# Output-projection weights in chunk order: fewer loads, an earlier first half, turned rows in other PSUM banks, and a reworked end

## Chip, core and metric

The kernel runs on one core of a Trainium2 chip. The metric is device time in microseconds (us) of one execution; lower is better. A core has five engines with an instruction queue each: TensorE (PE, matrix products), VectorE (DVE), ScalarE (ACT), GpSimd (POOL) and SyncE (SP, which here only issues DMAs). Each engine works through its queue in order, and waits on semaphores for what the other engines or DMAs must have done.

## What is computed

The reference runs one transformer-like layer over two batches, a prompt of 512 tokens and a sample of 1024 tokens, with shared weights. Cut to what matters:

```python
h = rmsnorm(x, norm_attn_g)
z = h @ w_in                              # 1024 -> q, k, v, conv a, conv b
a_out = window_attn(q, k, v, bias, sink)  # 8 heads of 64, 2 key heads, |q-k| <= 128
c = ca * sigmoid(cb); c = dwconv31(c); c = silu(layernorm(c))
x = x + concat(a_out, c) @ w_out          # 1024 x 1024
h = rmsnorm(x, norm_ffn_g)
u = dwconv3(h @ w_up)                     # 1024 -> 2 x 2816
x = x + (silu(u[:, :2816]) * u[:, 2816:]) @ w_down
y = rmsnorm(x, norm_final_g)
```

All data is 32-bit. Every product is made from three matmuls: each operand is split into a rounded part `hi` and a rest `lo`, and hi·hi, hi·lo and lo·hi are added in PSUM. A split is one ScalarE copy (`hi`) and one subtraction on VectorE or GpSimd (`lo`).

## The kernel before

**The stages, in order of time.** First comes the input projection (its last matmul ends near 282 us), in chunks of 128 output columns; `order` lists the chunks, those from index `npr` on only for the sample (`nt` 1 and 2). Beside it, a generator `prompt_attention` (L792) runs the prompt's attention in 8 units of one block and one key head, and after it the depthwise convolution's norm. Then `prompt_out` (L798) does the prompt's output projection with `w_out` and turns the normed rows of the prompt (`make_h2`, L773; `transposed`, L236), with the first units of the sample's attention advanced between its steps. The prompt's feed-forward part follows (its last matmul at 785 us), with the sample's attention beside it, then the sample's output projection, and from about 874 us the sample's feed-forward part, written as products of 2 x 2 blocks with seven products instead of eight: up-projection in `NJ` = 22 steps (loop at L1584), down-projection in groups of 11 steps (`down_step`, L1556), and at last the final norm (`finish`, L1525).

**What sets the order.** On most stretches a planner orders each engine's queue: it simulates the instructions with a cost model and takes what is ready, by the order of the program. In the sample's feed-forward part the order of TensorE (from L1601 on also of SyncE) is that of the program (`manual_schedule`), two such blocks meeting at L1602.

**Memory.** SBUF tiles come from `Slots` (L64): named slots of fixed size, 15 of 4 KB (`q`), 4 of 4.25 KB (`c`), 61 of 2 KB (`h`), 2 of 2.25 KB (`d`). A tile gets the first free slot of the smallest size that fits, and a slot goes to the end of the list when its tile is dropped in the program. A new tile's first write waits until the last reader of the slot's earlier tile is done. PSUM is handed out the same way from 8 banks: `a0` to `a2`, `u0`, `u1`, `b0`, `b1`, `c0`; `use` says which job may take which letters. Before `prompt_out` it is set as at L830:

```python
    use.update(attn="a", norm="b", turn="ab")
```

so that turned rows (`turn`) share the `a` banks with the attention, while `out_half` takes `u` banks, and the units before it took `a` or `u`.

**Loads of `w_out`.** `load_wo(kc, n)` (L747) loads 128 rows by 512 columns of chunk `kc`, half `n`, into a 2-KB slot. For `kc` < 4 the rows of the two key heads lie apart, so there are two DMAs of 64 rows (L753); for the others one (L755). `split_wo` (L757) splits a chunk by L153 (ScalarE) and L154. `prompt_out` loads the eight chunks of a half, splits them, and runs `out_half` (L717) for each of the four blocks: per chunk three matmuls, L727 to L729, then the addition of the residual (L732) and, after half 1, the sum of squares (L739) and the scale (L137, L138). `make_h2` scales the rows (L778); `transposed` makes four transposes per 128 columns (L240) into one bank, which ScalarE (L242) and VectorE (L243) read out.

**An attention unit** (`values`, L613): `turn` transposes probabilities (L625) into a bank, ScalarE and VectorE split them from there (L627, L628); the products are L639 and L640; the result is read out by L647, L648 (ScalarE) and L649 (VectorE), and GpSimd adds the two halves (L651).

**The last up-projection step** (`j` = 21) runs seven products of 12 matmuls each (`prod`, L1156): `second`, `sixth` (its result is copied out at L1243), `seventh` (it adds to the bank that L1243 reads), the first down step's 12 matmuls, `fourth` (into a bank that ScalarE has filled with `seventh`'s result, L1252), `third`.

**The end.** For the last two row blocks (`tt` 2 and 3) of the sample, `left_first` squares the left half in advance. After the last matmul, VectorE adds the product to the rest (L1641 by way of `add`, L1036), ScalarE sums the squares (L1530), GpSimd finishes the sum (L1532) and takes the power -1/2 (L1533), VectorE and ScalarE scale the halves (L1542, L1540), and SyncE issues both stores, one after the other (L1543).

Of the kernel before, what the change touches and what calls it, by code (L numbers as in the profile page):

```python
# [99 lines left out]
def tile_hybrid_encoder(ctx: ExitStack, tc: tile.TileContext, xs, rel_bias, norm_attn_g, w_in,  # L100
# [70 lines left out]
    def want_w(i):  # L171
        if i < nch and i not in ws:
            want_raw(i)
            ws[i] = split(raws.pop(i))

# [332 lines left out]
    def load_bias(n):  # L508
        b0 = bbd[:]
        for h in range(0, NH, n):  # L510
            bt = sb.tile([n, 3 * P])
            for e in range(n):
                nc.sync.dma_start(bt[:, e, :], bass.AP(b0.tensor, b0.offset + (h + e) * NT + P - 1, [[NH * NT - 1, P], [1, 3 * P]]))
                bias.append((bt, e))
# [232 lines left out]
    def load_wo(kc, n):  # L747
        raw = wor[kc, n] = sb.tile([NT])
        s = slice(n * NT, (n + 1) * NT)
        if kc < 4:  # L750
            for kv in range(NKV):
                r0 = (kv * GRP + kc) * HD
                nc.sync.dma_start(raw[kv * HD:(kv + 1) * HD, :], w_out[0, r0:r0 + HD, s])  # L753
        else:
            nc.sync.dma_start(raw[:], w_out[0, kc * P:(kc + 1) * P, s])  # L755

    def split_wo(kc, n, dve=False):  # L757
        wo[kc, n] = split(wor.pop((kc, n)), dve)
# [63 lines left out]
    for i in range(npr, nch):  # L822
        want_raw(i + 2)
        want_w(i + 1)
        for nt in range(1, 3):
# [4 lines left out]
    use.update(attn="a", norm="b", turn="ab")  # L830
# [286 lines left out]
    class Part:  # L1117
        def __init__(self, held, n):
            self.held, self.n = held, n

        def __getitem__(self, i):
            return self.held[:, self.n, :][i]

# [100 lines left out]
    def armed(out):  # L1224

        hi, lo = A[1, 0]
# [241 lines left out]
    def mm_down(out, i, p, tt):  # L1468
        (sh, sl), (th, tl) = hl[i, p]
        c = slice(tt * P, (tt + 1) * P)  # L1470
        nc.tensor.matmul(out, sh[:, c], th[:], start=(p == 0), stop=False)  # L1471
        nc.tensor.matmul(out, sh[:, c], tl[:], start=False, stop=False)  # L1472
        nc.tensor.matmul(out, sl[:, c], th[:], start=False, stop=(p == NPAIR - 1))  # L1473
# [44 lines left out]
    def left_first(tt):  # L1518

        ss, o = early[tt] = sm(2), sb.tile([D])  # L1520
        part = cut(o11, tt)
        nc.scalar.activation(o[:, L], part, AF.Square, accum_out=ss[:, 0:1])
        nc.vector.tensor_tensor(part, part, fins[0][:, L], op=ALU.mult)

    def finish(blk, parts, tail):  # L1525
        ss, o = early.pop(blk) if tail else (sm(2), sb.tile([D]))
        rs = sm(2)
        for n in range(1 if tail else 0, 2):
            s = slice(n * NT, (n + 1) * NT)
            nc.scalar.activation(o[:, s], parts[n], AF.Square, accum_out=ss[:, n:n + 1])  # L1530
        nc.gpsimd.tensor_scalar(rs[:, 0:1], ss[:, 0:1], 1.0 / D, EPS, op0=ALU.mult, op1=ALU.add)
        nc.gpsimd.tensor_scalar(rs[:, 1:2], ss[:, 1:2], 1.0 / D, rs[:, 0:1], op0=ALU.mult, op1=ALU.add)  # L1532
        nc.gpsimd.tensor_tensor(rs[:, 1:2], rs[:, 1:2], nhalf[:, 0:1], op=ALU.pow)  # L1533
        for n in range(2):
            s = slice(n * NT, (n + 1) * NT)
            if n == 0 and not tail:
                nc.scalar.activation(o[:, s], parts[n], AF.Identity, scale=rs[:, 1:2])
                nc.gpsimd.tensor_tensor(o[:, s], o[:, s], fins[0][:, s], op=ALU.mult)
            elif n == 0:
                nc.scalar.activation(o[:, s], parts[n], AF.Identity, scale=rs[:, 1:2])  # L1540
            else:
                nc.vector.scalar_tensor_tensor(o[:, s], parts[n], rs[:, 1:2], fins[0][:, s], op0=ALU.mult, op1=ALU.mult)  # L1542
            nc.sync.dma_start(GR[1]["o"][blk * P:(blk + 1) * P, s], o[:, s])  # L1543
# [168 lines left out]
```

## Times and profile before

| | |
|---|---|
| median of 3 runs | 1525.64 us (1525.16 to 1525.9) |
| the profiled execution's own time | 1529.8 us |
| its span, from first to last instruction | 1528.0 us |
| VectorE busy | 1177.5 us (77%) |
| ScalarE busy | 801.6 us (52%) |
| GpSimd busy | 742.9 us (49%) |
| DMA queue of SyncE, share of 16 engines | 41.0% |

How to read it: the times of the three runs are without the profiler; the profile is of a further execution. Engine times are the union of an engine's instructions. In a timeline row stand the start, the time from the start to the end of the last of the merged instructions, the engine, the line, the operation and how many; in square brackets is how long the engine had been idle before, and which instruction ended the wait. "SPq" is a DMA issue. Tile names are those of the slots (`q`, `h`, `c`, `d`) or banks (`a`, `u`, `b`, `w`), without numbers.

### The profile page before, as it was taken

The page shows a single profiled execution, that of the slowest core. Times are in us where ns is not written, and L with a number is a line of the kernel's source. Part 1 is how long each engine was busy: PE and PEld are TensorE (multiplying, and loading weights), DVE is VectorE, ACT ScalarE, POOL GpSimd, SP SyncE. Part 2 cuts the span into 40 slices and gives each one's busy share as a digit, 9 for nine tenths or more (in the row PEclk, how much of TensorE's full clock was granted, in tenths as well). Part 3 has the DMA queues.
Part 4 walks back from the last instruction along what each step waited for, and adds up shares of the span by engine and source line. Part 5 has one row for each costly group of instructions (what it writes and reads, how often), then busy time and mean ns, then how long its engine had stood idle before and what let it go on. Part 6 is the DMA issues. An engine that isn't in the chain of part 4 may idle for free. (4 is left out here: it accounts for less than half of the span.)

```text
span 1528.0 us, 20034 instructions
## 1 busy us (share of the span) xinstructions
PE 1492.7 (98%) x6800; PEld 1226.7 (80%) x6800; DVE 1177.5 (77%) x1669; ACT 801.6 (52%) x1414; POOL 742.9 (49%) x648
## 2 busy tenths in 40 slices
PE   8999999899999999999999999999999999999997
PEld 7888777787888877878878888888888888788886
DVE  7877847558799989995575878888888877886794
ACT  6424454467566565665355365444444445454364
POOL 3454353228677777786542325555555554000236
PEclk9999999999999999999999999999999999999999
DMA  9455231834333333345474213333333323585642
GB/s 376 154 165 150 85 104 35 254 112 124 97 111 100 123 102 109 102 128 173 141 243 140 83 56 104 103 104 103 104 104 104 103 90 127 207 341 167 205 145 110
DMA packets 106754, 209.71 MB, mean 137 GB/s; under 512 B 11507, under 2 KB 31091, under 8 KB 106524
## 3 DMA queue, kind: packets, MB, share of 16 engines
q1 hardware_dynamic: 105404, 207.36, 41.0%
q8 instruction: 53, 0.87, 0.2%
q10 hardware_dynamic: 1248, 1.09, 0.2%
q14 instruction: 49, 0.40, 0.1%
HBM read 161.98 MB, written 47.46 MB: 137 GB/s over the span
## 5 line engine op out<-in xcount | busy, mean ns | idle before, releaser
L1039 POOL TENSOR_TENSOR q<-q,q 128x512 fp32r<-128x512 f32 x82 | 114.4, 1407 | 155.8 <-ACT q L1148 151.9
L154 POOL TENSOR_TENSOR q<-q,q 128x1024 fp32r<-128x1024 f32 x66 | 159.9, 2425 | 58.2 <-ACT q L153 21.2
L281 PE MATMUL u<-h,q 128*128 128x512 f32 x384 | 151.8, 395 | 1.3 <-DVE h L890 0.9
L282 PE MATMUL u<-h,q 128*128 128x512 f32 x384 | 150.5, 392 | 0.0
L283 PE MATMUL u<-h,q 128*128 128x512 f32 x384 | 150.2, 391 | 0.0
L1162 PE MATMUL w<-h,q 128*128 128x512 f32 x372 | 146.3, 393 | 2.4 <-ACT h L1243 1.5
L1164 PE MATMUL w<-h,q 128*128 128x512 f32 x372 | 144.9, 390 | 0.7 <-POOL q L1039 0.7
L322 DVE SCALAR_TENSOR_TENSOR c<-c,cvw,c 128x512 f32<-128x512 f32 x184 | 137.4, 747 | 1.7
L1163 PE MATMUL w<-h,q 128*128 128x512 f32 x350 | 136.3, 389 | 0.0
L1036 POOL TENSOR_TENSOR q<-q,q 128x1024 f32<-128x1024 f32 x8 | 23.9, 3001 | 180.8 <-DVE q L1036 169.4
L153 ACT CAST q<-q 128x1024 fp32r<-128x1024 f32 x66 | 69.1, 1050 | 67.6 <-POOL q L154 39.8
L1471 PE MATMUL w<-h,h 128*128 128x512 f32 x264 | 102.7, 389 | 0.0
L1473 PE MATMUL w<-h,h 128*128 128x512 f32 x264 | 102.7, 389 | 0.0
L1039 DVE TENSOR_TENSOR h<-h,h 128x512 fp32r<-128x512 f32 (+1 forms) x128 | 92.2, 762 | 11.1 <-ACT h L1043 9.0
L1039 POOL TENSOR_TENSOR c<-q,c 128x512 fp32r<-128x512 f32 x46 | 72.1, 1580 | 49.8 <-ACT c L1148 49.8
L1472 PE MATMUL w<-h,h 128*128 128x512 f32 x244 | 95.0, 390 | 0.0
L314 POOL TENSOR_TENSOR h<-h,h 128x512 f32<-128x512 f32 x57 | 76.1, 1335 | 28.4 <-ACT h L313 23.5
L1043 ACT CAST h<-h 128x512 fp32r<-128x512 f32 x101 | 58.7, 619 | 58.0 <-DVE h L1039 30.5
L1162 PEld LDWEIGHTS w<-h,q 128*128 128x128 f32 x372 | 69.8, 188 | 20.6 <-ACT w L1234 3.6
L281 PEld LDWEIGHTS u<-h,q 128*128 128x128 f32 x384 | 72.1, 188 | 16.9 <-DVE h L890 2.1
L154 POOL TENSOR_TENSOR h<-h,h 128x512 fp32r<-128x512 f32 x52 | 70.4, 1360 | 29.2 <-ACT h L153 19.7
L283 PEld LDWEIGHTS u<-h,q 128*128 128x128 f32 x384 | 72.1, 188 | 15.0 <-POOL q L154 0.4
(445 smaller groups left out, 4364.7 us busy)
## 6 DMA issues: line engine op xcount, KB each, us to landing
q<-in_laid_w_up SPq DMA_DIRECT2D x88, 512.0 KB, 3.6
h<-in_w_down SPq DMA_DIRECT2D x90, 256.0 KB, 3.6
ga<-q SPq DMA_DIRECT2D x64, 256.0 KB, 2.0
h<-ga SPq DMA_DIRECT2D x57, 256.0 KB, 3.9
q<-in_laid_w_in SPq DMA_DIRECT2D x22, 512.0 KB, 3.9
q<-in_x_sample SPq DMA_DIRECT2D x15, 512.0 KB, 6.0
h<-qsd SPq DMA_DIRECT2D x24, 256.0 KB, 3.3
qsd<-h SPq DMA_DIRECT2D x44, 128.0 KB, 2.4
```

Source lines behind the costliest of these rows:

```text
L154: (nc.vector if dve else nc.gpsimd).tensor_tensor(lo[:], raw[:], hi[:].bitcast(F32), op=ALU.subtract)
L281: nc.tensor.matmul(out, whi[:, kc, :], hi[:], start=(kc == 0), stop=False)
L282: nc.tensor.matmul(out, whi[:, kc, :], lo[:], start=False, stop=False)
L283: nc.tensor.matmul(out, wlo[:, kc, :], hi[:], start=False, stop=(kc == KC - 1))
L322: nc.vector.scalar_tensor_tensor(acc[:], src(t), w(t), acc[:], op0=ALU.mult, op1=ALU.add)
L1039: (eng or nc.vector).tensor_tensor(out, a, b, op=ALU.subtract)
L1162: nc.tensor.matmul(out, whi[:, s], hi[:], start=(start and c == 0), stop=False, **go)
L1163: nc.tensor.matmul(out, whi[:, s], lo[:], start=False, stop=False, **go)
L1164: nc.tensor.matmul(out, wlo[:, s], hi[:], start=False, stop=(stop and c == 3), **go)
L1471: nc.tensor.matmul(out, sh[:, c], th[:], start=(p == 0), stop=False)
L1472: nc.tensor.matmul(out, sh[:, c], tl[:], start=False, stop=False)
L1473: nc.tensor.matmul(out, sl[:, c], th[:], start=False, stop=(p == NPAIR - 1))
```

## The change

- The host hands over `w_out` in a second layout, [half, 128 rows, chunk, 512 columns], with the two key heads' rows of a chunk already beside each other. `load_wo` is one DMA for every chunk; the new `load_wo_pair` loads two chunks with one DMA of 512 KB into a 4-KB slot.
- In the loop over the last projection chunks, at the last chunk, the first four chunks of half 0 are loaded as two pairs. `prompt_out` then loads only the other four of that half.
- From `prompt_out` on, turned rows take banks `u`, `b`, `c` and no longer `a`.
- Two heads' bias rows come with one DMA instead of two (L513), and the two copies of the keys likewise (L765).
- In the last up-projection step, `fourth` and `third` run before `seventh`. `fourth` starts its bank anew; `seventh`'s result is copied out by ScalarE and added to `fourth`'s by VectorE; `y_sum` follows the first down step.
- At the end, for `tt` 2 and 3, the part to be added is copied into the PSUM bank before the products (behind a matmul, `armed`, that opens the bank), so that the products add to it; the left half's sum of squares is put as a root into one more PSUM column behind the right half, so that one ScalarE instruction over 513 columns gives the whole sum; the factor 1024 goes into the final weights; one GpSimd instruction is left; the left half's store is issued by ScalarE's queue.

The diff, cut to its core:

```diff
     def load_wo(kc, n):
         raw = wor[kc, n] = sb.tile([NT])
-        s = slice(n * NT, (n + 1) * NT)
-        if kc < 4:
-            for kv in range(NKV):
-                r0 = (kv * GRP + kc) * HD
-                nc.sync.dma_start(raw[kv * HD:(kv + 1) * HD, :], w_out[0, r0:r0 + HD, s])
-        else:
-            nc.sync.dma_start(raw[:], w_out[0, kc * P:(kc + 1) * P, s])
+        nc.sync.dma_start(raw[:], laid["w_out"][n, :, kc, :])
+
+    def load_wo_pair(kc, n):
+        both = sb.tile([2, NT])
+        nc.sync.dma_start(both[:], laid["w_out"][n, :, kc:kc + 2, :])
+        for m in range(2):
+            wor[kc + m, n] = Part(both, m)
...
             for L in range(2):
-                for half in range(2):
-                    nc.sync.dma_start(kt[1, kv][L][half * HD:(half + 1) * HD, :].bitcast(F32), ksd[:, kv, L, :])
+                k = ksd[:, kv, L, :]
+                nc.sync.dma_start(kt[1, kv][L][:].bitcast(F32), bass.AP(k.tensor, k.offset, [[0, 2]] + list(k.ap)))
...
     for i in range(npr, nch):
         want_raw(i + 2)
         want_w(i + 1)
+        if i == nch - 1:
+            for kc in range(0, 4, 2):
+                load_wo_pair(kc, 0)
         for nt in range(1, 3):
             step(i, nt)
         ws.pop(i)
     h1.clear()
     rbs.clear()
-    use.update(attn="a", norm="b", turn="ab")
+    use.update(attn="a", norm="b", turn="ubc")
...
+        last = j == NJ - 1
         value_part(j - 1)
+        if last:
+            fourth(j, None, True)
+            third(j)
         first(j + 1)
         split_up(j + 1, 6)
-        seventh(j)
-        if j == NJ - 1:
+        seventh(j, None, not last)
+        if last:
...
             down_step(0)
         fifth(j + 1)
         split_up(j + 1, 7)
-        fourth(j)
+        if last:
+            y_sum(j)
+        else:
+            fourth(j)
         gate_part(j)
         split_up(j + 1, 4)
-        third(j)
+        if not last:
+            third(j)
...
-    def left_first(tt):
-
-        ss, o = early[tt] = sm(2), sb.tile([D])
+    def left_first(tt, z):
+
+        ss, o = early[tt] = sm(2), sb.tile([D + 4])
         part = cut(o11, tt)
-        nc.scalar.activation(o[:, L], part, AF.Square, accum_out=ss[:, 0:1])
+        squares(ss, 0, part, o[:, L])
+        nc.gpsimd.tensor_tensor(ss[:, 0:1], ss[:, 0:1], half[:], op=ALU.pow)
+        nc.scalar.copy(z[:, NT:NT + 1], ss[:, 0:1])
         nc.vector.tensor_tensor(part, part, fins[0][:, L], op=ALU.mult)
...
     def finish(blk, parts, tail):
         ss, o = early.pop(blk) if tail else (sm(2), sb.tile([D]))
...
+        if tail:
+            nc.scalar.activation(o[:, NT:D + 1], parts[2], AF.Square, accum_out=ss[:, 1:2])
...
+        nc.gpsimd.tensor_tensor(rs[:], ss[:, 1:2], nhalf[:, 0:1], op=ALU.pow)
+        for n in (1, 0):
...
-            nc.sync.dma_start(GR[1]["o"][blk * P:(blk + 1) * P, s], o[:, s])
+            (nc.scalar if n == 0 and tail else nc.sync).dma_start(GR[1]["o"][blk * P:(blk + 1) * P, s], o[:, s])
...
             nc.sync.dma_start(fins[0][:], norm_final_g.partition_broadcast(P))
+            nc.scalar.activation(fins[0][:], fins[0][:], AF.Identity, scale=D ** 0.5)
...
+        if p == 4:
+            for tt in (2, 3):
+                zs.append(wide())
+                armed(zs[-1][:, L], hl[3, p][0][0])
+                nc.scalar.copy(zs[-1][:, L], cut(o12, tt))
...
     for tt in (2, 3):
-        left_first(tt)
-        z = wide()
+        z = zs.pop(0)
+        left_first(tt, z)
         for p in range(NPAIR):
-            mm_down(z[:, L], 3, p, tt)
-        add(cut(o12, tt), z[:, L], cut(o12, tt))
-        finish(tt, (cut(o11, tt), cut(o12, tt)), True)
+            mm_down(z[:, L], 3, p, tt, True)
+        finish(tt, (cut(o11, tt), z[:, L], z[:, 0:NT + 1]), True)
```

More of the change, by code (lines that the diff above doesn't have):

```diff
@@ L174, in want_w, with __init__, __getitem__ @@
             ws[i] = split(raws.pop(i))
+    class Part:
+        def __init__(self, held, n):
+            self.held, self.n = held, n
+        def __getitem__(self, i):
+            return self.held[:, self.n, :][i]
     class Halves:
@@ L1622, in tile_hybrid_encoder @@
     base = len(steps) - NPAIR
+    zs, half = [], sm(1)
+    nc.gpsimd.memset(half[:], 0.5)
     z = wide()
```

60 lines of the change are left out of this document (30 added, 30 removed).

## The prediction

> **What bounds the kernel now.** The page comes first.
>
> ```profile
> span 1528.0 us, 20034 instructions
> PE 1492.7 (98%) x6800; PEld 1226.7 (80%) x6800; DVE 1177.5 (77%) x1669; ACT 801.6 (52%) x1414; POOL 742.9 (49%) x648
> ```
>
> TensorE is busy for all but 35.3 us of the span. The change removes no matmul, so it can only win TensorE's waits, slow stretches and the end behind its last matmul; no other engine's busy time counts unless TensorE waits for it. So I looked for the waits in the places that the diff touches, by windows.
>
> ```profile
> core 0: us, PE busy (x) PEld busy (x) DVE busy (x) ACT busy (x) POOL busy (x), PEclk, DMA share, GB/s
> 282.00:288.50 6.50, 1.24 (x10) 0.90 (x8) 4.48 (x8) 4.22 (x9) 4.29 (x3) 0.88 0.96 310
> 288.50:293.90 5.40, 5.36 (x13) 4.23 (x14) 4.68 (x9) 3.85 (x9) 1.08 (x2) 0.51 0.93 265
> 341.00:355.00 14.00, 10.68 (x60) 7.22 (x60) 9.34 (x18) 12.53 (x24) 10.91 (x10) 1.00 0.34 107
> 1299.00:1312.00 13.00, 10.93 (x48) 8.39 (x47) 13.00 (x19) 8.22 (x13) 0.00 (x0) 1.00 0.43 155
> ```
>
> Three holes: 5.3 us before the first output projection, after which TensorE's granted clock is about half for 5.4 us; 3.3 us where the prompt's rows are turned; 2.1 us in the last up-projection step. The timeline of the first hole (rows of several engines, in order of time):
>
> ```profile
> 273.78 5.52 SPq L753 DMA_DIRECT2D h<-in_w_out  x8
> 276.76 0.39 PE L640 MATMUL a<-q,h 128*128 128x512 f32 x1
> 280.38 0.62 ACT L153 CAST h<-h 128x512 fp32r<-128x512 f32 x1 [6.81 <-PE b L283]
> 281.02 0.58 ACT L647 COPY q<-a 64x512 f32<-64x512 f32 x1
> 282.25 0.68 DVE L649 TENSOR_TENSOR q<-a,h 64x512 f32<-64x512 f32 x1 [0.52 <-ACT h L648]
> 282.85 3.08 DVE L154 TENSOR_TENSOR h<-h,h 128x512 fp32r<-128x512 f32 x5
> 283.01 4.04 POOL L651 TENSOR_TENSOR q<-q,q 64x512 fp32r<-64x512 f32 x1 [5.22 <-DVE q L649]
> 287.09 0.59 ACT L627 CAST q<-u 128x512 fp32r<-128x512 f32 x1 [2.28 <-POOL q L651]
> 287.70 0.69 DVE L628 TENSOR_TENSOR q<-u,q 128x512 fp32r<-128x512 f32 x1 [1.77 <-ACT q L627]
> 288.54 0.76 PE L727 MATMUL u<-h,h 128*128 128x512 f32 x1 [5.31 <-DVE q L628]
> 291.24 0.63 PE L727 MATMUL u<-h,h 128*128 128x512 f32 x1
> 293.80 0.41 PE L727 MATMUL u<-h,h 128*128 128x512 f32 x1
> ```
>
> Read from the bottom: TensorE waits 5.31 us for L628 to empty the `u` bank that the output projection is to take over from an attention unit. L627 ahead of it waited for GpSimd's L651, since its output goes to the slot that L651 reads (`q` in both rows). L651 waited for L649, and that for L647, whose input TensorE had finished at 276.76 + 0.39 = 277.15. ScalarE took it up only at 281.02, because its queue stood 6.81 us at the first split of `w_out`. The releaser named there had long ended; what came last were the half-chunk loads, issued from 273.78 on. So late weights hold the bank, by way of the engine's order. From 288.54 to 293.80 there are 12 matmuls in 5.26 us.
>
> **The change, part by part.**
>
> *First half of w_out (A).* Full pace, from twelve matmuls of the last up-projection step, and that step's waits:
>
> ```profile
> 1300.80 0.57 ACT L1243 COPY h<-w 128x512 f32<-128x512 f32 x1
> 1301.42 0.50 PE L1162 MATMUL w<-h,q 128*128 128x512 f32 x1 [1.46 <-ACT h L1243]
> 1305.64 0.39 PE L1162 MATMUL w<-h,q 128*128 128x512 f32 x1
> 1308.14 0.39 PE L1164 MATMUL w<-h,q 128*128 128x512 f32 x1
> 1309.14 0.50 PE L1162 MATMUL w<-h,q 128*128 128x512 f32 x1 [0.61 <-DVE w L1036]
> ```
>
> From 1305.64 to 1308.14 are eleven steps: 0.227 us each. Twelve at full pace take 2.73 us, so the slow clock cost 5.26 - 2.73 = 2.53, and A can win 5.31 + 2.53 = 7.84 us at most. How much, the slots decide; durations of loads and of L651:
>
> ```profile
> L651 POOL TENSOR_TENSOR h<-h,h x21: 1262/1292/1767, 158.1 to 714.6; 64x512 fp32r<-64x512 f32 x21
> h<-in_w_out SPq DMA_DIRECT2D x16, 256.0 KB, 4.5
> q<-in_laid_w_up SPq DMA_DIRECT2D x88, 512.0 KB, 3.6
> q<-in_x_prompt SPq DMA_DIRECT2D x8, 512.0 KB, 6.3
> L1543 SPq DMA_DIRECT2D out_sample<-q x16: 332/358/410, 1506.8 to 1524.8; - x16
> ```
>
> I followed the first-free rule through the program's order. At the last chunk the two pairs get the first two free 4-KB slots. The first pair's slot was last read by the L640 that ends at 277.15; the second pair's by the L651 above. In exchange the attention unit in the `u` bank gets slots that two projection weights have left, so L627 and L628 no longer wait for L651, and the bank is free some 2 us after its transposes, before 281. So the pairs come hardly earlier than the old loads, but the chain to the bank is cut. What is late next is chunk 0, then chunk 2. Chunk 0: issue 0.36 (L1543's row), landing taken as 4.5 (between 3.6 and 6.3, the two kinds of 512 KB): 282.0; `hi` at 282.6, `lo` at 283.3. TensorE is free at 288.54 - 5.31 = 283.23: no wait (1.2 us with 6.3). Chunk 2: L647 now starts at 277.15, if ScalarE takes it before the split, and it is ready before any load that waits for the same L640 can land; with L648 and L649 that is 279.0, with L651 at its usual 1.29 it is 280.3, issue and landing 285.2, `hi` 285.8. TensorE wants it six matmuls after 283.23, at 284.6: 1.2 us of wait, some 0.4 more for `lo`; with 6.3 us of landing 3.4 in all. I take 2.5 left over: A = 7.84 - 2.5 = 5.3, from 0 to 7.8.
>
> The clock: the window 288.50:293.90 behind a hole of 5.31 us stands at 0.51; 341.00:355.00, with holes of up to 2.31 us (below), at 1.00. My two waits lie below the lower one. [...]
>
> *Turned rows (B).*
>
> ```profile
> 344.76 0.69 DVE L628 TENSOR_TENSOR h<-a,h 128x512 fp32r<-128x512 f32 x1 [2.26 <-ACT h L627]
> 345.37 0.74 DVE L778 TENSOR_SCALAR q<-q,rs 128x1024 f32<-128x1024 f32 x1
> 345.43 5.90 POOL L314 TENSOR_TENSOR h<-h,h 128x512 f32<-128x512 f32 x4 [0.24 <-ACT h L310]
> 345.51 0.55 PE L240 MATMUL a<-ident,q 128*128 128x128 f32 x3 [2.31 <-DVE h L628]
> 351.98 2.40 POOL L154 TENSOR_TENSOR q<-q,q 128x1024 fp32r<-128x1024 f32 x1 [0.52 <-PE b L240]
> 354.44 0.51 PE L283 MATMUL u<-h,q 128*128 128x512 f32 x1
> ```
>
> The 2.31 us are a bank `a` that the attention still held. With banks of their own the turned rows don't wait there; but the fourth block's scaled row is ready only at 345.37 + 0.74 = 346.11, so only the three other blocks' transposes move ahead. The next limit is the `lo` of the first up-projection weights: L154 starts when the last transposes free its slot, and L283 follows its end. With five banks in turn those transposes come earlier, but GpSimd's queue is busy to 345.43 + 5.90 = 351.33, so L154 gains 0.65 unless the planner puts it ahead. I take B = 1.0; ends: 3.3 (the whole hole) and -0.5 (the up-projection's `u` banks wait for turned rows).
>
> *Last step (C).* `fourth` and `third`, 24 matmuls or 5.4 us, come between `sixth` and `seventh`. `sixth` ended near 1298.4, so `seventh` would start near 1303.9, while L1243 ends at 1301.37: the 1.46 us go. The 0.61 stood before `third`, which now follows `fourth` and has no addition ahead: C = 2.1. Added is one VectorE addition of 0.7 us where VectorE is full (13.00 of 13.00 us); the cover is the stock of split operands, since from 1312 on TensorE did not wait. If that is too thin, 0.7 to 1.0 comes back: C from 1.0 to 2.1.
>
> *The end (D).*
>
> ```profile
> 1521.17 0.68 DVE L1036 TENSOR_TENSOR q<-w,q 128x512 f32<-128x512 f32 x1
> 1521.89 0.63 ACT L1530 ACTIVATE q<-q 128x512 f32<-128x512 f32 x1 [0.67 <-DVE q L1036]
> 1522.71 0.27 POOL L1532 TENSOR_SCALAR s<-s,s 128x1 f32<-128x1 f32 x1 [2.24 <-ACT q L1530]
> 1523.06 0.55 POOL L1533 TENSOR_TENSOR s<-s,nhalf 128x1 f32<-128x1 f32 x1
> ```
>
> The addition goes (1521.17 to 1521.89: 0.72), L1532 goes (0.35), and the second store no longer queues behind the first on SP (0.36): 1.43. Two `armed` matmuls come before the end, 0.45. D = 1.0, from 0.3 (if ScalarE's issue costs more than SP's) to 1.4. The copies into PSUM run beside the first two row blocks' products, which don't need them.
>
> *The rest at nothing:* fewer issues for biases, keys and the sample's `w_out` (SP's queue was behind no TensorE wait but A's), and one ScalarE scaling of the final weights (ScalarE 52% busy). The planner may order other stretches anew; I allow 1.3 us either way, the size of the one wait
>
> ```profile
> PE b L281 <- DVE h L400: 1.3, 1, 1.3
> ```
>
> Sum: 5.3 + 1.0 + 2.1 + 1.0 = 9.4. The profiled execution took 1529.8 us, 1.8 more than its span, so it would take 1520.4; the median of the runs is 4.2 lower, 1525.6, which gives **1516.2 us**.
>
> **Rivals.**
>
> *Half stays (0.20).* L651 takes 4.04 us again, not 1.29, because VectorE splits beside it: chunks 4 to 7 get 2-KB slots that were free early, so their splits fall just there. For: the 4.04 row with five L154 beside it. Against: VectorE may split earlier or later. The second pair is then 2.75 us later, and the wait is 1.6 + 2.75 = 4.4 to 6.2, near the one that halved the clock: A about 0, time 1521.5. [...]
>
> *Slower: ScalarE stands before the split again (0.07).* If the planner puts chunk 0's split ahead of L647, L651 starts after the first pair has landed, and the second pair after L651: two landings in series. With 4.5 us each: 282.0 landed, 282.6 split, 283.8 L648, 284.5 L649, 288.6 L651 (4.04), 293.4 landed, 294.0 `hi`. TensorE is at chunk 2 at 294.0, not 291.24, with all 2.53 us of slow clock to come, of which half (1.3) lay behind it before: 4.1 lost, less C and D (3.1): 1526.6. With 6.3 each it is 1530.2. From 5.5 us of landing on it is slower beyond what can be measured; middle 1528.5. Against it: L647 is ready over 4 us before chunk 0 can have landed.
>
> *Little of it carries (0.11).* Orders shift elsewhere, C or D is eaten by later waits: 1519 to 1526, middle 1523.
>
> **How the numbers follow.** The forecast has 0.62. About 0.2% of the time, 3.05 us, is what a measurement here can tell from no change: faster is below 1522.6, slower above 1528.7. Faster: 0.62 + 0.8 x 0.20 + 0.4 x 0.11 = 0.82; slower 0.55 x 0.07 + 0.2 x 0.11 = 0.06; the same 0.12. Range: low end with A 7.8, B 1.8, C 2.1, D 1.4, 13.1 in all, and half of the 1.3: 1512.0; high end 1523.0, which takes in the first rival and half of the last.
>
> **What would show it.** Right: L627 of the unit before the output projection not behind L651; the hole there under 3.4 us, the clock 1.00 behind it; a second short wait at the seventh matmul; no `a` bank among the turned rows; no wait at `seventh`; about 5.4 us from the first instruction that reads the last product to the end of the span (before, 1521.17 to 1528.0). Wrong: a first-split row on ScalarE with a long wait ahead of L647, a load of a pair issued after 285, or new waits between 380 and 1280 us.

## The result, and the profile after

| | kernel before | changed kernel |
|---|---|---|
| median of 5 runs | 1525.64 us (1525.01 to 1526.8) | 1559.2 us (1556.22 to 1562.59) |
| ratio to before, 95% interval | | 1.0223 [1.0205, 1.0241] |
| profiled execution, its span | 1529.8 us, 1528.0 us | 1558.9 us, 1557.1 us |

The changed kernel is 33.6 us slower, where 9.4 us of gain were forecast. Its line numbers are up to 13 higher than those of before: the output projection's matmuls are L733 to L735 (L727 to L729 before), the key loads L774 (L765), the scores' matmul L589 (L583). First the page of the profile after:

```profile
span 1557.1 us, 19999 instructions
PE 1491.7 (96%) x6802; PEld 1226.9 (79%) x6802; DVE 1176.8 (76%) x1668; ACT 804.0 (52%) x1419; POOL 743.8 (48%) x649
```

TensorE's busy time is that of before within 1 us, and its idle time went from 35.3 to 65.4 us. So a wait was added, and TensorE's waits name it (who waits for whom: total us, times, longest):

```profile
PE a L589 <- DMA q<-ksd: 35.4, 1, 35.4
PE b L940 <- DVE q L943: 3.0, 2, 1.5
PE w L1477 <- ACT h L1055: 1.0, 1, 1.0
```

One wait of 35.4 us: the first scores of the sample's attention wait for the keys that are loaded back from DRAM (`ksd`). The windows around it (columns as in the prediction: five engines, granted clock, DMA share, GB/s):

```profile
281.00:288.00 7.00, 7.00 (x33) 5.74 (x32) 6.58 (x11) 5.16 (x10) 3.15 (x5) 1.00 0.66 209
293.00:298.00 5.00, 0.99 (x5) 0.49 (x3) 0.00 (x0) 0.00 (x0) 0.00 (x0) 0.84 0.13 52
298.00:303.00 5.00, 0.00 (x0) 0.00 (x0) 0.00 (x0) 0.00 (x0) 0.00 (x0) 0.50 0.13 52
308.00:313.00 5.00, 0.00 (x0) 0.00 (x0) 0.00 (x0) 0.00 (x0) 0.00 (x0) 0.50 0.13 52
315.00:318.00 3.00, 0.00 (x0) 0.00 (x0) 0.00 (x0) 0.00 (x0) 0.00 (x0) 0.50 0.94 341
323.00:334.00 11.00, 4.36 (x13) 3.52 (x14) 1.90 (x7) 1.59 (x6) 0.00 (x0) 0.50 0.27 92
334.00:340.00 6.00, 6.00 (x31) 5.05 (x30) 3.07 (x10) 1.44 (x5) 0.20 (x1) 1.00 0.06 16
```

No engine computes from 298 to 323 us. From 298 to 303 and from 308 to 313 us the DMA engines are busy for 0.13 of their time, as if two of sixteen (0.125) worked, at 52 GB/s. Between and behind these windows other loads run beside the keys, and from 315 to 318 us the share is 0.94: there was room, but the keys alone did not use it. The four key loads are 2 MB, which at 52 GB/s is 40 us. The issues, from the timeline of SyncE:

```profile
277.25 0.59 SPq L774 DMA_DIRECT2D q<-ksd  x1
286.30 6.74 SPq L774 DMA_DIRECT2D q<-ksd  x2
293.09 9.66 SPq L566 DMA_DIRECT2D h<-qsd  x1
302.85 1.03 SPq L774 DMA_DIRECT2D q<-ksd  x1
303.96 10.82 SPq L142 DMA_DIRECT2D q<-in_x_prompt  x3
```

The queue is held up too: one issue of L566 takes 9.66 us while the key loads are under way, and the residual rows (L142) come late with it. And the clock is at half from 296.4 to 334.0 us, so the first matmuls after the wait run at about half pace: each begins 0.43 us after the one before it, and from 334.0 us on 0.23.

What the prediction was mostly about did happen. The first hole, in the timeline of several engines:

```profile
281.28 1.66 ACT L766 CAST h<-h 128x512 fp32r<-128x512 f32 x3 [0.24 <-DMA h<-in_laid_w_out]
281.78 0.39 PE L733 MATMUL u<-h,h 128*128 128x512 f32 x1
284.53 0.58 ACT L653 COPY h<-a 64x512 f32<-64x512 f32 x1
287.22 1.28 POOL L657 TENSOR_TENSOR q<-q,h 64x512 fp32r<-64x512 f32 x1 [3.58 <-DVE q L655]
```

The output projection starts at 281.78 us without any wait, where it started at 288.54 before, and TensorE is busy for 7.00 of the 7.00 us from 281 on. GpSimd's addition takes 1.28 us, not 4.04. The hole is gone, but the wait that followed cost far more.

The end, against 1521.17 to 1528.0 before:

```profile
1551.25 0.60 ACT L1542 ACTIVATE c<-w 128x513 f32<-128x513 f32 x1 [5.00 <-PE w L1479]
1552.02 0.55 POOL L1547 TENSOR_TENSOR s<-s,nhalf 128x1 f32<-128x1 f32 x1 [6.53 <-ACT c L1542]
1552.60 0.72 ACT L1551 ACTIVATE c<-q,s 128x512 f32<-128x512 f32 x1 [0.66 <-POOL s L1547]
1553.35 0.38 ACTq L1556 DMA_DIRECT2D out_sample<-c  x1
```

From the first reader of the last product to the end of the span it is 5.85 us (1551.25 to 1557.1); before it was 6.83. The forecast was 5.4.

### The profile page after: what moved, and what is told of

It is laid out like the page before. It is cut to its first block, busy times and chain, and to the rows that moved or that the text cites. A ratio compares the mean times of both kernels' runs of the same rounds, so it can differ in the third digit from the quotient of the medians.

```text
span 1557.1 us, 19999 instructions
## 1 busy us (share of the span) xinstructions
PE 1491.7 (96%) x6802; PEld 1226.9 (79%) x6802; DVE 1176.8 (76%) x1668; ACT 804.0 (52%) x1419; POOL 743.8 (48%) x649
## 5 line engine op out<-in xcount | busy, mean ns | idle before, releaser
L602 ACT ACTIVATE h<-h,s 128x385 f32<-128x385 f32 (+1 forms) x95 | 55.1, 580 | 88.1 <-DVE s L593 84.7
```

## The theories

Theory E: a load gets as many of the 16 DMA engines as its source's first count says, and the source of the new key loads begins with a count of 2 (`[0, 2]`). It was read off the trace, which has a share of 0.13 (two of sixteen are 0.125) at 52 GB/s in two windows of the wait; whether the count sets it was for the experiments to show. Its rivals: R, reading each row twice, or the load's size, is slow; O, the scores' place in TensorE's queue is at fault, so that any load is late. Beside them stood the question what the rest of the change is worth without the keys. The kernel before ran again beside each set of experiments; its median there was 1526.6 to 1527.2 us, and each ratio is to the runs of the same set.

A trace is of one execution, and that lay up to 5.5 us from its kernel's median (the one of the kernel before 4.2 us above it). In the four kernels with the same code up to the end of `prompt_out` (before, and later the end alone, the last step alone and both) TensorE idles 4.30 to 5.76 us from 280 to 320 us. So the windows show where the waits stand; a difference of about 1 us in that stretch shows nothing, and what a part is worth in all is told by the ratios.

## The experiments on the keys

**Old key loads in the changed kernel.**

```diff
-                nc.sync.dma_start(kt[1, kv][L][:].bitcast(F32), bass.AP(k.tensor, k.offset, [[0, 2]] + list(k.ap)))
+                for half in range(2):
+                    nc.sync.dma_start(kt[1, kv][L][half * HD:(half + 1) * HD, :].bitcast(F32), ksd[:, kv, L, :])
```

> The changed kernel with the keys loaded as before, by eight DMAs of 64 rows instead of four with a twofold source. Theory E (the twofold source makes the transfer run on two of the sixteen DMA engines: in the wait the profile shows a DMA share of 0.13 at 52 GB/s): the 35.4 us wait at the first sample scores goes, and with it some 3 to 6 us of halved clock: 1559.2 - 35.4 - 5 = about 1518, and the DMA share in that stretch is over 0.3. Theory O (the scores' place in TensorE's queue is at fault: the planner puts them 16 us earlier than before, so that any load is late): a wait of over 5 us stays there, 1523 or more.

Measured: 1528.43 us, ratio 1.0007 [0.9998, 1.0016]. The 31 us are gone with the form of these loads, and the wait that stays at the scores is 3.18 us, so O falls too. But the gain that was expected of the rest is not there. What TensorE and VectorE wait for after the hole that was closed:

```profile
296.98 1.62 PE L589 MATMUL a<-q,h 128*128 128x256 f32 x6 [3.18 <-DMA q<-ksd]
299.94 0.69 DVE L738 TENSOR_TENSOR q<-u,q 128x512 f32<-128x512 f32 x1 [7.04 <-DMA q<-in_x_prompt]
300.69 0.80 PE L733 MATMUL u<-h,h 128*128 128x512 f32 x1 [1.67 <-DVE q L738]
```

TensorE waits 3.18 us for the keys and, at 300.69, 1.67 us for an addition that itself waited 7.04 us for the residual rows. Two things make these rows late: without the hole the addition is due earlier, and their loads stand further back in SyncE's queue. The first one, in the kernel before and in this one:

```profile
280.04 0.36 SPq L142 DMA_DIRECT2D q<-in_x_prompt  x1
```

```profile
291.28 0.34 SPq L142 DMA_DIRECT2D q<-in_x_prompt  x1
```

It is issued 11.2 us later, behind the key loads, which now come earlier. From 280 to 320 us TensorE idles 4.85 us, against 5.31 before.

**The new key loads alone**, in the kernel before.

```diff
-                for half in range(2):
-                    nc.sync.dma_start(kt[1, kv][L][half * HD:(half + 1) * HD, :].bitcast(F32), ksd[:, kv, L, :])
+                k = ksd[:, kv, L, :]
+                nc.sync.dma_start(kt[1, kv][L][:].bitcast(F32), bass.AP(k.tensor, k.offset, [[0, 2]] + list(k.ap)))
```

> The kernel before with the twofold source of the keys' loads alone. Theory E: four loads of 512 KB at 52 GB/s take 40 us in series, so TensorE waits 25 to 40 us at the first sample scores: 1550 to 1570. Theory O (order, not the loads): within 5 us of before, 1521 to 1531.

Measured: 1557.62 us, ratio 1.0197 [1.0183, 1.0211]. Half as many issues cost 30 us by themselves. While TensorE still works, a window shows the same share, 0.13 at 52 GB/s:

```profile
305.00:310.00 5.00, 5.00 (x24) 4.17 (x24) 1.42 (x3) 2.09 (x5) 1.47 (x2) 1.00 0.13 52
```

The price is paid in two places: the output projection waits 10.6 us (5.3 before), since the issues of eight half-chunk loads, queued behind the first key load, take 10.86 us in place of 5.52; and later the scores stand for 18.6 us (the profile names no releaser there).

**The same number of rows in 16 groups.** Each load walks 16 groups of 8 rows, 3 rows apart, so that most rows are still read two or three times; the sample's keys are therefore not the reference's.

```diff
-bass.AP(k.tensor, k.offset, [[0, 2]] + list(k.ap))
+bass.AP(k.tensor, k.offset, [[3 * row, 16], [row, 8], cols])
```

> The changed kernel, four loads as in it, but each source written as 16 groups of 8 rows, the groups 3 rows apart (128 rows read out of 53, so most rows are read two or three times; the sample's keys are thereby other rows than the reference's). Theory E: the first dimension is 16, all engines carry it: as the version with eight loads, within 2 us, about 1518. Theory R (reading the same rows of memory more than once is what is slow, or one DMA of 128 rows into both halves): the wait stays, 1545 or more.

Measured: 1526.6 us, ratio 1.0004 [0.9995, 1.0013], the wait for the keys 3.2 us. So four loads of 512 KB with overlapping rows are not what cost the 35.4 us. R falls.

**The dose: 4 groups of 32 rows**, 10 rows apart (again other keys than the reference's).

```diff
-bass.AP(k.tensor, k.offset, [[0, 2]] + list(k.ap))
+bass.AP(k.tensor, k.offset, [[10 * row, 4], [row, 32], cols])
```

> The changed kernel with the keys' source walked as 4 groups of 32 rows, 10 rows apart, in place of 2 groups of 64 (other rows of keys than the reference's, the same bytes and the same number of loads). Theory E (the number of DMA engines that a load gets is the source's leading count): 4 of 16 engines, DMA share near 0.25 and some 105 GB/s in the stretch in which only the keys move, the wait of the first scores matmul for the keys 10 to 18 us in place of 35.4, the time 1535 to 1545 us. Rival 2 (a leading count of 2 alone is slow): the wait near 3 us, as with 16 groups, the time within 2 us of 1526.6.

Measured: 1543.95 us, ratio 1.0114 [1.0099, 1.0128]. First TensorE's wait, then the window around its end:

```profile
PE a L589 <- DMA q<-ksd: 19.2, 1, 19.2
```

```profile
310.00:314.00 4.00, 1.84 (x7) 1.58 (x8) 0.97 (x2) 0.00 (x0) 0.00 (x0) 0.50 0.26 105
```

Counts of 2 and 4 give shares of 0.13 and 0.26, and 52 and 105 GB/s; counts of 2, 4 and 16 give waits of 35.4, 19.2 and 3.2 us. The wait is a little over the range that was given (10 to 18); the share is as expected. Theory E stands for these three counts.

**Keys stored twice**, so that four plain loads of 128 rows do it.

```diff
-    ksd = dr.tile([HD, NKV, 2, 1024], F32, name="ksd")
+    ksd = dr.tile([P, NKV, 2, 1024], F32, name="ksd")
...
-                        nc.sync.dma_start(ksd[:, kv, L, cols], src_k)
+                        for half in range(2):
+                            nc.sync.dma_start(ksd[half * HD:(half + 1) * HD, kv, L, cols], src_k)
...
+                nc.sync.dma_start(kt[1, kv][L][:].bitcast(F32), ksd[:, kv, L, :])
```

> The changed kernel with the sample's keys stored to memory twice (eight more stores of 128 KB, in the first 160 us) and loaded by four plain DMAs of 128 rows. Theory E: no wait at the first scores; as the version with eight loads or up to 1.5 us better, since four issues less stand in SP's queue: 1516 to 1519. Theory R: the same, since no row is read twice; so this one tells E and R apart only together with the 16 groups. Theory O: a wait of over 5 us stays, 1523 or more.

Measured: 1526.22 us, ratio 0.9995 [0.9986, 1.0003]. TensorE is busy for all 40.00 us from 280 to 320 us, at clock 1.00. That is more than A's forecast: the 5.31 us of wait and the slow clock are all gone, and yet the time is the same. Elsewhere it idles more: 3.67 us from 400 to 440 us, where it idled 0.0 before, 0.9 more from 120 to 160 (where the stores were doubled), 0.6 more from 200 to 240. This does not add up to the whole: the execution in the trace is 6.0 us shorter than that of the kernel before (1522.0 against 1528.0), the median only 0.85. What takes the rest of the gain in the other executions is not shown.

## The parts one by one

**The end alone** (D), the hunks of `squares`, `left_first`, `finish` and `armed` in the kernel before:

```diff
+                armed(zs[-1][:, L], hl[3, p][0][0])
+                nc.scalar.copy(zs[-1][:, L], cut(o12, tt))
...
-            mm_down(z[:, L], 3, p, tt)
-        add(cut(o12, tt), z[:, L], cut(o12, tt))
+            mm_down(z[:, L], 3, p, tt, True)
```

> The kernel before with the reworked end alone (D). By the forecast's working: 1.0 us faster than before, 0.3 to 1.4. Rival (the seeding costs TensorE a wait before the last blocks, or the store from ScalarE's queue lands later): 0 to 1 us slower. In its profile the time from the first reader of the last product to the end of the span tells: 5.4 us by the forecast, 6.8 in the kernel before; in the version with eight key loads it was 5.8.

Measured: ratio 0.9987 [0.9978, 0.9996], 2.0 us faster (0.6 to 3.4). The forecast of 1.0 lies inside. The trace of the changed kernel shows 0.98 behind the last product (6.83 to 5.85), where the forecast had 1.43.

**The last up step alone** (C):

```diff
+        if last:
+            fourth(j, None, True)
+            third(j)
         first(j + 1)
         split_up(j + 1, 6)
-        seventh(j)
+        seventh(j, None, not last)
```

> The kernel before with the new order of the last up-projection step alone (C). Forecast: the waits of 1.46 and 0.61 us go, 2.1 us faster. New theory, from the version with eight key loads (there the two waits are gone but 1.2 and 1.0 us appear at the down steps, behind splits of ScalarE and VectorE): the stock of split operands was the real limit there; the waits move by some 10 us and the time is the same within 0.5 us.

Measured: ratio 0.999 [0.9975, 1.0005], which settles nothing by itself. The windows do: TensorE's idle time falls from 2.44 to 0.35 us from 1280 to 1320 us, and from 1320 to 1360 us 0.85 us are new, 0.6 of them a down product that waits for a split operand. That is 1.2 us net. The other traces agree: of the kernels here within 0.4% of the one before, those with the old order idle 0.0 us from 1320 to 1360 us, those with the new one 0.57 to 1.51.

**Both together**, the two edits above in the kernel before:

> The kernel before with the last up step's order and the end alone. Alone the end gave 0.9987 and the last step 0.9990. Theory AD (they touch different waits and add up): ratio 0.9977, about 3.5 us faster. Rival OV (the last step only moves its wait to 1320 to 1360 us and gains nothing by itself): ratio 0.9987, 2 us.

Measured: 1525.04 us, ratio 0.9983 [0.9974, 0.9992], 2.6 us faster. Its interval holds both what adding up gives (0.9977) and what the end gives alone (0.9987), so the time does not decide between the theories. The windows do, for the waits: from 1280 to 1360 us TensorE idles 1.60 us against 2.44, so C keeps some 0.8 us beside D.

**`w_out` alone** (A), with the turned rows left in banks `a` and `b`:

```diff
+        nc.sync.dma_start(raw[:], laid["w_out"][n, :, kc, :])
...
+        if i == nch - 1:
+            for kc in range(0, 4, 2):
+                load_wo_pair(kc, 0)
```

> The kernel before with w_out in the second layout, one load per chunk and the two early pairs alone (A): keys, banks, last step and end as before. Forecast: the hole before the output projection shrinks to 2.5 us in short waits, the clock stays: 5.3 us faster. New theory (what is late next is the keys' loads, which the first sample scores need, since TensorE now reaches them earlier): a wait of 3 to 5 us at the scores and a halved clock behind it: 0 to 1.5 us faster.

Measured: 1530.5 us, ratio 1.0018 [1.0008, 1.0027]: 2.7 us slower. Its timeline (line numbers one higher than in the changed kernel) shows that the pairs come late:

```profile
276.56 0.76 SPq L760 DMA_DIRECT2D q<-in_laid_w_out  x1
280.80 0.38 SPq L760 DMA_DIRECT2D q<-in_laid_w_out  x1
284.72 1.14 ACT L767 CAST h<-q 128x512 fp32r<-128x512 f32 x2 [2.46 <-DMA q<-in_laid_w_out]
285.39 0.49 PE L734 MATMUL u<-h,h 128*128 128x512 f32 x1 [2.82 <-ACT h L767]
```

In the changed kernel they were issued at 268.94 and 272.79 us; here at 276.56 and 280.80, behind the loads of the other chunks. So TensorE waits 2.82 us for the first split, and later 3.6 us for an addition whose residual rows came late. From 280 to 320 us it idles 6.85 us.

**The banks alone** (B):

```diff
-    use.update(attn="a", norm="b", turn="ab")
+    use.update(attn="a", norm="b", turn="ubc")
```

> The kernel before with the turned rows in banks u, b, c alone (B). Forecast: 1.0 us faster, between 3.3 faster and 0.5 slower. New theory (the waits of 3 to 4 us that the versions with mended keys show between 360 and 440 us, behind the prompt's down-projection, come from these banks): 1 to 4 us slower, with such waits. Third theory (they come from the other parts' shift of the planner's order): no such waits here, and 0 to 2 us faster.

Measured: 1532.81 us, ratio 1.0035 [1.0023, 1.0048]: 5.3 us slower. The wait of 2.3 us in front of the turned rows is gone, but others stand in its place and the stretch from 320 to 360 us idles 2.93 us (3.32 before). And from 400 to 440 us, in the prompt's down-projection, it idles 3.58 us. That stretch before, and with the banks alone:

```profile
400.00:440.00 40.00, 40.00 (x188) 33.33 (x187) 31.26 (x54) 24.88 (x44) 31.48 (x25) 1.00 0.35 112
```

```profile
400.00:440.00 40.00, 36.42 (x167) 29.20 (x166) 38.67 (x63) 23.83 (x43) 26.75 (x22) 1.00 0.32 106
```

VectorE's work went from 31.26 to 38.67 us of 40, and TensorE waits for it: 1.5 us for an addition (L931) and 2.0 us in the sample's attention (L649, L587). The same windows for the convolution's line alone (L322: VectorE busy, count), before and with the banks alone:

```profile
400.00:440.00 40.00, 8.99 (x12) 1.00 0.35 112
```

```profile
400.00:440.00 40.00, 17.19 (x23) 1.00 0.32 106
```

Eleven more of the convolution's taps stand there, each 0.75 us. One word for the banks has made the planner put other work into this stretch. That is 3.6 of the 5.3 us; where the rest comes from is not shown.

## What takes A's gain, and the better kernel

**Keys twice, banks `a` and `b`**, which leaves out B:

```diff
-    use.update(attn="a", norm="b", turn="ubc")
+    use.update(attn="a", norm="b", turn="ab")
```

> The changed kernel with the keys stored twice and read by four plain loads, and with the turned rows back in the banks a and b (as before): everything of the change but its banks and its twofold key source. Theory BK (the banks u, b, c for the turned rows bring the waits of the prompt's down-projection): the idle time of 400 to 440 us, 3.67 us with the same kernel and the banks u, b, c, falls below 1 us, and the whole is 3 to 5 us faster than the kernel before, ratio 0.997 to 0.998. Rival SH (the load of the w_out chunks and the late residual rows shift the order whatever the banks are): 280 to 320 us idles again by 4 to 7 us, as with the w_out part alone in the banks a and b (6.85), and the ratio is 0.999 to 1.001.

Measured: 1532.02 us, ratio 1.0033 [1.0021, 1.0045]. Half of each theory held: 400 to 440 us idles 0.0, and the pairs come late again (278.68 and 282.34 us, 3.09 us idle from 280 to 320). But new idle time stands from 520 to 680 us, 7.3 us against 3.6 before; 4.8 us of it are waits for VectorE and ScalarE in the sample's attention. Why the order is worse just there was not settled, and neither was whether this makes the median 5.0 us longer: the spans of the two traces are the same (1527.8 and 1528.0 us).

**The residual rows ahead of the keys.** The whole change but its banks and its key loads (so banks `a` and `b`, old key loads), and the rows of two blocks loaded first in the program:

```diff
     use.update(attn="a", norm="b", turn="ab")
+    for i in range(2):
+        xr[i] = load_x(*blocks[i])
     load_kv()
```

> w_out, the last step and the end of the change on the kernel before: banks a and b, the eight key loads of before, and the residual rows of the first two prompt blocks loaded ahead of the keys. With the w_out part alone the residual add waited 7.0 us for these rows' load, and TensorE 3.6 us for that add. Theory XR (the hole that w_out's loads left is the rows' and keys' place in the queue): the residual add waits for no load, 280 to 320 us idles below 4 us, ratio 0.996 to 0.998. Rival SP2 (the late splits and keys set it): the add's wait is gone but TensorE still idles 4 us or more there, for the split or the keys; ratio 0.999 to 1.001.

Measured: 1522.99 us (1520.89 to 1525.67), ratio 0.9974 [0.9965, 0.9984], beside 1527.06 for the kernel before: 4.1 us faster, the lowest ratio of all kernels here, though its interval overlaps with those of several others, the last step with the end (0.9983) among them. Its window and, behind it, the same places of its timeline:

```profile
280.00:320.00 40.00, 37.44 (x170) 29.54 (x170) 24.96 (x55) 22.26 (x53) 6.04 (x13) 0.96 0.72 219
```

```profile
284.14 0.49 PE L733 MATMUL u<-h,h 128*128 128x512 f32 x1 [1.92 <-ACT h L766]
300.52 0.50 PE L733 MATMUL u<-h,h 128*128 128x512 f32 x1 [0.28 <-DVE q L738]
```

TensorE waits 0.28 us for the addition instead of 3.6, and 1.92 us for the first split. It idles 2.56 us in this stretch. On SyncE's queue the planner still puts the first two key loads ahead of the rows; the rows' first load is issued at 285.66 us (287.25 with `w_out` alone), the last at 292.43 (297.92). The next addition still waits 2.11 us for its rows, but TensorE does not wait for that one.

**The rows alone, and `w_out` with the rows:** the edit above in the kernel before, then on top of `w_out` alone (neither with the last step or the end).

> The kernel before with the residual rows of the first two prompt blocks loaded ahead of the keys, and nothing else. Theory XR (rows and w_out only pay together: in the kernel before the hole of 280 to 320 us ends at the split of w_out, not at a row): 280 to 320 us idles as before (4 to 6 us) and the ratio is 0.999 to 1.001. Rival RO (the rows' place is worth it by itself): ratio 0.9985 or less.

> The w_out part alone (banks a and b, eight key loads) with the residual rows of the first two prompt blocks loaded ahead of the keys. Theory XR: the 2.7 us by which the w_out part alone was slower turn into a gain, ratio 0.9985 to 0.9995, idle of 280 to 320 us at 2 to 4 us (6.85 without the rows). Rival: the gain of the best kernel so far (0.9974) is that of the last step and the end alone (0.9983), and w_out with rows is at 1.000 or above.

Measured: the rows alone 1.0011 [1.0, 1.0022], with 5.25 us idle from 280 to 320; `w_out` with the rows 0.9995 [0.9984, 1.0006], with 2.62 us. So the rows turn 2.7 us of loss into 0.8 us of gain, which can't be told from none. By the medians, most of the best kernel's gain is C and D (2.6 us).

Part of why A brings so little even so is the clock. The stretch from 280 to 320 us before, and with `w_out` and the rows:

```profile
280.00:320.00 40.00, 34.69 (x160) 28.79 (x159) 25.15 (x55) 24.75 (x57) 9.92 (x14) 0.91 0.72 221
```

```profile
280.00:320.00 40.00, 37.38 (x163) 29.23 (x163) 25.20 (x54) 22.89 (x54) 6.72 (x14) 0.91 0.69 215
```

The wait before the output projection fell from 5.31 to 2.0 us, but the granted clock is 0.91 in both; in the kernel before it was at half from 287.0 to 293.8 us. In the best kernel, behind a wait of 1.92 us, it was at half from 284.9 to 288.4, 0.96 in the stretch. A mean of 0.91 is 3.6 us short of full pace in 40 us (0.09 x 40), and what of it falls into the wait costs nothing; in the kernel before, 2.53 us fell on matmuls. So with `w_out` and the rows the slow clock still costs some 3 us (an estimate from these figures).

**Three rows instead of two**, in the best kernel:

```diff
-    for i in range(2):
+    for i in range(3):
         xr[i] = load_x(*blocks[i])
```

> The best kernel so far with the rows of three blocks loaded ahead of the keys in place of two. In that kernel the residual add still waits 2.1 us for a row's load, while TensorE waits 0.3 us for that add and 1.9 us for a split. Theory: worth nothing more, ratio 0.997 to 0.998; rival (the third load pushes keys and w_out back in the queue): 280 to 320 us idles over 4 us, ratio 0.999 or more.

Measured: 1528.67 us, ratio 1.0016 [1.0005, 1.0026]. From 280 to 320 us it idles 3.96 us, and from 520 to 680 us 6.4 us, as with the keys stored twice. The rival was nearer, but the larger part of the new idle time is again that later stretch.

**The banks of the turned rows in the best kernel:** `u`, `b`, `c`; then `u`, `b`; then `a`, `b`, `c`.

```diff
-    use.update(attn="a", norm="b", turn="ab")
+    use.update(attn="a", norm="b", turn="ubc")
```

> The best kernel so far (w_out, last step, end, rows first; 0.9974 with the banks a and b) with the turned rows in the banks u, b, c, as the change has them. Theory BK: the waits in the prompt's down-projection come back, 400 to 440 us idles 3 to 4 us (0.0 in a and b), and the time is 3 to 5 us longer, ratio 1.000 to 1.001. Rival: those waits come with another order of the work and not with the banks; then the ratio stays within 0.001 of 0.9974.

> The best kernel so far (w_out, last step, end, two rows first) with the turned rows in the banks u and b. Theory CB (it is the bank c, shared with the depthwise convolution, that makes the planner order the work anew): as with a and b, the pairs of w_out are issued near 276 and 280 us, the convolution has 12 to 14 taps of VectorE in 400 to 440 us, TensorE idles 0.0 there, ratio 0.997 to 0.998. Rival AB (leaving the bank a does it): pairs near 268 and 272 us, 23 to 24 taps, 3.6 us idle.

> The best kernel so far with the turned rows in the banks a, b and c. Theory CB: as with u, b and c, the pairs of w_out are issued near 268 and 272 us, 23 to 24 taps of the convolution in 400 to 440 us, TensorE idles 3.6 us there, ratio 0.998 to 1.000. Rival AB: as with a and b, pairs near 276 and 280 us, 12 to 14 taps, no idle time.

| banks | ratio to before | pairs issued at, us | taps in 400 to 440 us | TensorE idle there, us |
|---|---|---|---|---|
| a, b | 0.9974 [0.9965, 0.9984] | 276.72, 280.45 | 14 | 0.0 |
| u, b | 0.9989 [0.998, 0.9997] | 277.37, 281.40 | 10 | 0.0 |
| u, b, c | 0.9984 [0.997, 0.9999] | 267.51, 271.35 | 25 | 3.69 |
| a, b, c | 1.0012 [1.0, 1.0025] | 266.65, 270.49 | 25 | 1.66 |

Two rows of the table as the windows have them (the convolution's line alone), with `u` and `b`, and with `a`, `b` and `c`:

```profile
400.00:440.00 40.00, 7.36 (x10) 1.00 0.34 112
```

```profile
400.00:440.00 40.00, 18.57 (x25) 1.00 0.34 110
```

In these four, the order of the work follows bank `c`, in which the convolution accumulates, and not the leaving of `a`. With it, the pairs come 9 us earlier (which A needs) and the convolution's taps crowd the prompt's down-projection. The times followed neither theory: theory BK's wait of 3.69 us came back with `u`, `b`, `c`, but not its 3 to 5 us, and the ratios with `u`, `b` and with `a`, `b`, `c` lie above the ranges of theory CB. With `a`, `b` and `c` the idle time there was 1.66 us, below the 3.6 expected; 2.74 us more stand from 480 to 520. Which banks are better depends on the rest: with the keys stored twice `u`, `b`, `c` was the faster (0.9995 against 1.0033 with `a`, `b`), with the rows first `a`, `b` (0.9974 against 0.9984, intervals that overlap). What decides that is not shown. In all kernels here that are within 0.4% of the one before, the taps from 400 to 440 us number 23 to 26 with `c`, and 8 to 14 without. By which rule the planner comes to it was not traced.

## Why the prediction was wrong, step by step

- **The step that failed** is "*the rest at nothing:* fewer issues for biases, keys and the sample's `w_out`". The keys' four loads cost 31 us (1559.2 to 1528.43). They were counted in issues and bytes; the share of the DMA engines' time that one load gets (0.13, at 52 GB/s) was not looked at. No rival held this either. The reason given, that SP's queue was behind no TensorE wait but A's, was true of the loads of before only: the bound was taken from rows of another form of load.
- **A: 5.3 of 7.84.** The chain was read rightly, and the hole closed wherever the pairs came early. That it closed in the changed kernel was luck: there the pairs came 8 us earlier than the slots had told (268.94 and 272.79 us), by way of bank `c`, which the working did not connect with them. In the best kernel, without `c`, the slots were read well: pairs at 276.72 and 280.45 (read as 277 and 280.3), 2.2 us of waits left over (2.5), though 1.92 of them for the first split (0 to 1.2) and none at the second pair.
- **A, what is late next** was followed only to the second pair. The residual rows and the keys were next, and took gain back: without the rows ahead, 2.7 us slower; with them, 0.8 us faster (between 2.4 faster and 0.9 slower).
- **A, the clock.** The 2.53 us of slow clock were counted as won because the waits left over would lie below 2.31 us, a wait behind which one trace showed 1.00. That bound does not hold, and nor do the 3.4 us of "What would show it": from 280 to 320 us the clock was 0.96 with a wait of 1.92 us (the best kernel) and 0.91 with one of 2.0 (`w_out` with the rows). And from 320 to 360 us, with 3.20 to 3.32 us idle and the same code, it was 1.00 in two traces (before, the end alone) and 0.96 in two others (the last step alone, and both). The stretch of the last of these:

```profile
320.00:360.00 40.00, 36.69 (x177) 30.14 (x176) 20.20 (x40) 25.57 (x48) 20.80 (x23) 0.96 0.42 121
```

- **B: 1.0, wrong sign.** The wait for bank `a` did go, as said, but the choice of banks also orders the work: alone it cost 5.3 us. The lower end of -0.5 held only the banks' direct price, and "1.3 us either way" for new orders was too small; 3.6 us stood in one stretch alone.
- **C: 2.1.** The two waits went; 0.85 us came back further on (forecast as 0.7 to 1.0, if the stock of split operands was too thin). The lower end, 1.0, was nearer than the value that was taken: 1.2 us by the windows.
- **D: 1.0.** The runs bear it out: 2.0 us (0.6 to 3.4). Its terms are less sure: behind the last product 0.98 us were won where 1.43 were worked out, and the 0.45 us for the two `armed` matmuls were not measured.
- Of the rivals, "little of it carries" describes the rest without the keys (1528.43 us, though outside its 1519 to 1526). Neither "half stays" nor ScalarE standing before the split was seen: GpSimd's addition took 1.28 us.

## What to carry to other kernels

When a DMA is merged or reshaped, look at the first count of its access pattern before counting issues and bytes (the runs here vary that of the source): the source that starts with 2 halved the key loads' issues and kept the DMA engines busy for 0.13 of their time, at 52 GB/s; TensorE waited 35.4 us for it, and 3.2 us with a first count of 16. Before giving a closed hole its full price, list the loads that are issued near it and ask which is late next, and don't count a slow clock as won because a shorter wait once went without it (one of 2.31 us did here, others of 1.92 and 2.0 did not). And under a planner a change of buffers or banks is a change of order as well: check far from the edit, and price it by trying it alone.

## What was not expected of the hardware

- The key loads' speed went with the first count of their source: 2 gave 0.13 of the DMA engines' time and 52 GB/s, 4 gave 0.26 and 105 GB/s.
- While the slow loads ran, the issue of later ones on the same queue took longer: one of L566 took 9.66 us (the median of that line, L560 in the kernel before, is 0.33 there), and three of the residual rows' loads 10.82 us (3.02 us in the kernel before).
- TensorE's clock fell to half 2.4 us into the wait of 35.4 us and stayed there until 334.0 us, 4.7 us after the matmuls had begun again.
- A single wait of 1.8 to 2.0 us before the output projection came with a slow clock too: 0.96 from 280 to 320 us in the best kernel (half clock from 284.9 to 288.4 us), and 0.91 in two others (`w_out` with the rows, and banks `u`, `b`), as much as in the kernel before with its wait of 5.31 us.
